# A separate byte offset for each stage's split activations in an fp32r matmul kernel

## The chip, the cores and the metric

The kernel runs on one core of a Trainium2 chip, in one launch. The metric is device time in microseconds. Before the change it is 2463.53 us, the median of two runs (2461.48 and 2465.57).

## What is computed

The reference runs two blocks, one after the other, on a sequence of 256 tokens with 1024 features in float32. The first block is a gated mixer (spatial gating, a depthwise convolution of width 31, a multi-scale pool) with a feed-forward layer. The second has two layers: a retention mixer and a latent attention mixer, each followed by a "peer" layer that scores all 16,384 experts densely in this kernel. Nearly all of the work is projections:

```python
proj = hn @ w_in[i]                                   # 1024 -> 8192
f_gate, f_up = jnp.split(hn @ w_ffn_in[i], 2, axis=-1)  # 1024 -> 2 * 2816
f = (jax.nn.silu(f_gate) * f_up) @ w_ffn_out[i]
...
q, k, v, g = jnp.split(x @ w_in, [RET_HK, 2 * RET_HK, 2 * RET_HK + RET_HV], axis=-1)
...
h = jax.nn.gelu(jnp.einsum('thkd,td->thk', u[eidx], xb), approximate=False)
return jnp.einsum('thk,thkd->td', gate * h, v[eidx])
```

## The kernel before

**Weights.** All weights are a list of 797 units of 128 x 1024 float32 in the order in which they are used (PLAN, L32). A unit comes from HBM into one of four `raw` buffers (issue_dma, L134), ScalarE copies it into one of three `whi` buffers as fp32r (issue_hi, L143), and VectorE subtracts the two into one of three `wlo` buffers (issue_split, L154). So a weight is a high part and a low part, both fp32r.

**Activations.** They are split in the same way into a high part `[:, 0]` and a low part `[:, 1]`, in a tile of 2 x 8 x 256 values (two halves of 8 KB in each partition, a k-step every 1 KB). The tile named `hl` lies in the pool `keep`, in one buffer with the tag "hl" that eight stages use in turn (new_hl, L441, and two tiles written out at L710 and L749).

**Two kinds of matmul.** A product is three matmuls: high x high, high x low, low x high.

- Feature-major stages (lin_fm, L234, and the expert loop at L1315) call mm3. The weight's 128 columns are the stationary operand, and a k-step of `hl`, 256 columns, streams through:

```python
220    def mm3(ps, w, x, start, stop):
...
222        nc.tensor.matmul(ps, w[0], x[0], start=start, stop=False, skip_group_check=True)
223        nc.tensor.matmul(ps, w[0], x[1], start=False, stop=False, skip_group_check=True)
224        nc.tensor.matmul(ps, w[1], x[0], start=False, stop=stop, skip_group_check=True)
```

- Token-major stages (lin_tm, L296) call tm_half. Here 128 columns of the activations are stationary and 512 columns of the weight stream:

```python
286        nc.tensor.matmul(ps[:, :n], xh, w[0][:, o:o + n], start=first, stop=False, skip_group_check=True)
287        nc.tensor.matmul(ps[:, :n], xh, w[1][:, o:o + n], start=False, stop=False, skip_group_check=True)
288        nc.tensor.matmul(ps[:, :n], xl, w[0][:, o:o + n], start=False, stop=last, skip_group_check=True)
```

Each matmul loads its own stationary operand (the rows of PEld), while the matmul before it streams.

**Addresses.** Pools are laid out by the sizes of their tiles. In each partition, `hl` begins at byte 14,848, which is 29 x 512. The weight buffers (`raw`, `whi`, `wlo`) begin at byte 32,320 and follow each other every 4,096 bytes; each lies 64 bytes past a multiple of 512. A weight's 128 columns are 512 bytes and a k-step of `hl` is 1,024, so modulo 512 the weight is always 64 bytes ahead of `hl`, in all stages. The other split tiles have places of their own: `fhl`, `yhl`, `ohl` and the expert loop's `ch` and `cl` lie 64 bytes past a multiple of 512, as the weights do; `hl2`, `hl4`, `hl5`, `hlp` and `cqhl` lie on one.

**What sets the order.** The order on every engine is that of the program text (manual_schedule); the only work between the matmuls of a stage is what `pump` (L170) takes from background generators. The stages that use `hl`, in order: w_conv, w_pin, w_u, w_v and w_gate (one tile), w_pgr, w_co, w_fi, then r_qk, r_v and r_g (one tile), then p_q0 with the 128 units of p_u0 (one tile), m_in, and p_q1 with p_u1 (one tile).

Of the kernel before, what the change touches and what calls it, by code (L numbers as in the profile page):

```python
# [11 lines left out]
F32R = mybir.dt.float32r  # L12
# [7 lines left out]
P = 128  # L20
T = 256
D = 1024
KD = D // P
# [69 lines left out]
def fused_kernel(ctx: ExitStack, tc: tile.TileContext, a: dict, out: bass.AP):  # L93
# [4 lines left out]
    keep = ctx.enter_context(tc.tile_pool(name="keep", bufs=1))  # L98
# [244 lines left out]
    def table_ready(func=AF.Sqrt):  # L343

        nc.scalar.activation(out=small("rt", 1), in_=eps_t[:, 0:1], func=func)
# [92 lines left out]
                nc.tensor.matmul(psb[b][k // 4][:, (k % 4) * P:(k % 4 + 1) * P], hm[:, k, b * P:(b + 1) * P], ident,  # L438
                                 start=False, stop=False, is_transpose=True, skip_group_check=True)

    def new_hl():  # L441
        return keep.tile([P, 2, KD, T], F32R, tag="hl", name="hl")

    class LnTail:

# [98 lines left out]
    issue_split(1)  # L544
    spread(dgs, bA)
    table_ready(AF.Sigmoid)
    hl = new_hl()
    hn32 = mx.tile([P, KD, T], F32, tag="hn32", name="hn32")

    def pr_x(k):  # L550
# [141 lines left out]
    def mk_branch(gi, first, last=None):  # L692
        def ev(f, ps):
            if first and f == 0:
                held["m"] = mx.tile([P, KD, T], F32, tag="v", name="merged")
            merged = held["m"]
            if first:
                nc.vector.tensor_tensor(out=merged[:, f, :], in0=ps, in1=gates[:, gi * 8 + f, :], op=ALU.mult)
                return
            t = tmp(mx, "brt")  # L700
            nc.vector.tensor_tensor(out=t, in0=ps, in1=gates[:, gi * 8 + f, :], op=ALU.mult)
            nc.vector.tensor_tensor(out=merged[:, f, :], in0=merged[:, f, :], in1=t, op=ALU.add)
            if last is not None and f > 0:
                late(f - 1)
        return ev
# [1 line left out]
    def late(f):  # L707
        split_to(hl5[:, 0, f, :], hl5[:, 1, f, :], held["m"][:, f, :])

    hl3 = keep.tile([P, 2, KD, T], F32R, tag="hl", name="hl3")  # L710
    br_s = mk_branch(0, True)

    def ev_sgo(f, ps):
# [18 lines left out]
    for gi in range(4):  # L732
        for f in range(2):
            c = 2 * gi + f
            gp = bank(c % 4)[:, :T]
            for k in range(2):
                t = gi * 4 + f * 2 + k
# [8 lines left out]
    drain_bg()  # L746


    hl3 = keep.tile([P, 2, KD, T], F32R, tag="hl", name="hl3b")  # L749
    cvt = {}  # L750

    def pr_conv1(c):
# [35 lines left out]
    lin_tm("w_out", of_fm(hl5), KD, after=rt1.after, warm=WRM)  # L788


    hl = new_hl()
    sqs = {}
    sqp = {}

# [117 lines left out]
    for f in range(8):  # L912
        for k in range(2):
            t = 2 * f + k
# [15 lines left out]
        split_to(hlp[:, 0, k, :], hlp[:, 1, k, :], h2[:, k, :])  # L930

    h3 = hm
    hl = new_hl()

    def ev_pleg(f, ps):
        t = ff.tile([P, T], F32, tag="ft", name="plt", bufs=3)
# [109 lines left out]
    ret_t(16)  # L1046
    ret_t(17)
    yl = rt.tile([P, 2, 1024], F32, name="yl")
    hl = new_hl()
    lt = LnTail(yl, "lm_g0", "lm_b0", hm, hl)  # L1050
    lin_tm("r_o", of_fm(yhl), 16, each=lambda k: 4 <= k < 8 and scale_h(k - 4), mid=add_h, after=lt.after, warm=WRM)

# [333 lines left out]
    def after0(X):  # L1386
        flat = X.rearrange("p a b -> p (a b)")
        y = flat[:, 0:2048].rearrange("p (b f) -> p b f", b=2)
        hl_ = new_hl()
        hl2_box["lt"] = LnTail(y, "lf_g0", "lf_b0", hm, hl_)  # L1390
        hl2_box["hl"] = hl_
        return hl2_box["lt"].after
# [5 lines left out]
    def angles():  # L1398
# [9 lines left out]
        yield from sincos(ang, sn2.rearrange("p b o f -> p (b o f)"), cs2.rearrange("p b o f -> p (b o f)"), keep, 64, 2.5, 2.5)  # L1408

    PE0, X = peer(0, hl, lt, [RT, TB], after0, beside_v=[angles()])  # L1410
    lt, hl = hl2_box["lt"], hl2_box["hl"]

# [171 lines left out]
            att_out(k + 1)  # L1584

    yl = ml.tile([P, 2, 1024], F32, name="yl")
    hl = new_hl()
    lt = LnTail(yl, "lm_g1", "lm_b1", hm, hl)
    lin_tm("m_o", of_fm(ohl), 8, each=att_each, mid=add_h, after=lt.after, warm=WRM)

# [142 lines left out]
```

## Time and profile before

| | us |
|---|---|
| median of the two runs | 2463.53 |
| the profiled execution | 2461.35 |
| its span, first to last instruction | 2459.3 |
| TensorE busy (PE) | 2423.2 |
| weight loads (PEld) | 2205.6 |
| VectorE busy | 1792.0 |
| ScalarE busy | 1285.0 |

The profile records for each matmul a start and a modelled end. In a stream, matmuls overlap, so that one lasts 276 ns or more while a new one starts every 113 ns or so; the distance from start to start is what the stream costs.

### The profile page before, as it was taken

Reading aid. Unit: us, or ns where it says so; the run is one execution under the profiler, and the core shown is the slowest. Engines: PE = TensorE matmul, PEld = TensorE weight load, DVE = VectorE, ACT = ScalarE, POOL = GpSimd, SP = SyncE. Lnnn points to the kernel's source line nnn. Section 1 sums busy time; section 2 is a strip of 40 time slices with the busy share of each in tenths; the row PEclk is TensorE's granted clock in tenths of the full one; section 3 lists DMA queues with packets and bytes.
Section 4 is the critical chain, followed back from the end, with each engine's and each line's share of the span. In section 5 each row is a group of like instructions: output and inputs, shape, how many; then the busy total and the mean of one; then the engine's idle time right before and its main releaser. Section 6 shows DMA issues by size and latency. Waiting matters only on the chain. (4 is left out here: it accounts for less than half of the span.)

```text
span 2459.3 us, 43069 instructions
## 1 busy us (share of the span) xinstructions
PE 2423.2 (99%) x16839; PEld 2205.6 (90%) x16839; DVE 1792.0 (73%) x3456; ACT 1285.0 (52%) x2175; POOL 4.9 (0%) x13
## 2 busy tenths in 40 slices
PE   8999999999999999999999999999999999999998
PEld 8899989889889999999878888779999999888886
DVE  7988767667657988889655555667978898555555
ACT  5444555564455555555455545645565555454554
POOL 0000000000000000000000000000000000000000
PEclk9999999999999999999999999999999999999999
DMA  6645555546354555545555555424555455655553
GB/s 205 221 143 172 180 161 189 189 163 197 127 182 165 175 188 176 172 164 172 188 188 194 192 196 183 135 86 164 191 195 166 168 168 172 213 191 194 196 191 128
DMA packets 119772, 432.66 MB, mean 176 GB/s; under 512 B 13808, under 2 KB 14192, under 8 KB 119184
## 3 DMA queue, kind: packets, MB, share of 16 engines
q1 hardware_dynamic: 118832, 425.84, 52.4%
q0 software_dynamic: 736, 4.06, 0.5%
q8 instruction: 132, 2.16, 0.3%
q14 instruction: 72, 0.59, 0.1%
HBM read 428.81 MB, written 1.05 MB: 175 GB/s over the span
## 5 line engine op out<-in xcount | busy, mean ns | idle before, releaser
L165 DVE TENSOR_TENSOR wlo<-raw,whi 128x1024 fp32r<-128x1024 f32 (+1 forms) x797 | 968.5, 1217 | 497.0 <-ACT whi L150 494.4
L150 ACT ACTIVATE whi<-raw 128x1024 fp32r<-128x1024 f32 (+1 forms) x797 | 839.8, 1055 | 686.0 <-PE bank L288 446.9
L222 PE MATMUL bank<-hl,whi 128*128 128x256 f32 x2080 | 586.0, 282 | 4.1 <-ACT hl L552 3.3
L223 PE MATMUL bank<-hl,whi 128*128 128x256 f32 x2080 | 578.6, 278 | 0.3
L224 PE MATMUL bank<-hl,wlo 128*128 128x256 f32 x2080 | 578.0, 278 | 0.3 <-DVE wlo L165 0.3
L286 PE MATMUL bank<-whi,ch 128*128 128x512 f32 x1024 | 398.9, 390 | 2.0 <-ACT ch L324 2.0
L288 PE MATMUL bank<-whi,cl 128*128 128x512 f32 x1024 | 398.8, 389 | 0.3 <-DVE cl L325 0.2
L287 PE MATMUL bank<-wlo,ch 128*128 128x512 f32 x1024 | 398.4, 389 | 0.0
L222 PEld LDWEIGHTS bank<-hl,whi 128*128 128x128 f32 x2080 | 392.6, 189 | 5.0 <-ACT hl L552 3.6
L223 PEld LDWEIGHTS bank<-hl,whi 128*128 128x128 f32 x2080 | 392.1, 189 | 1.4 <-DVE hl L467 0.5
L224 PEld LDWEIGHTS bank<-hl,wlo 128*128 128x128 f32 x2080 | 391.9, 188 | 1.2 <-DVE wlo L165 0.9
L222 PE MATMUL lps<-hl,whi 128*128 128x256 f32 x1208 | 342.6, 284 | 1.0 <-ACT fhl L836 0.6
L224 PE MATMUL lps<-hl,wlo 128*128 128x256 f32 x1208 | 336.8, 279 | 0.5 <-DVE wlo L165 0.5
L223 PE MATMUL lps<-hl,whi 128*128 128x256 f32 x1208 | 336.7, 279 | 0.0
L286 PEld LDWEIGHTS bank<-whi,ch 128*128 128x128 f32 x1024 | 192.2, 188 | 42.4 <-ACT ch L324 2.8
L288 PEld LDWEIGHTS bank<-whi,cl 128*128 128x128 f32 x1024 | 192.2, 188 | 41.9 <-DVE cl L325 1.9
L223 PEld LDWEIGHTS lps<-hl,whi 128*128 128x128 f32 x1208 | 229.0, 190 | 0.3
L222 PEld LDWEIGHTS lps<-hl,whi 128*128 128x128 f32 x1208 | 227.2, 188 | 1.8 <-ACT fhl L836 0.7
L224 PEld LDWEIGHTS lps<-hl,wlo 128*128 128x128 f32 x1208 | 227.0, 188 | 0.7 <-DVE wlo L165 0.7
L287 PEld LDWEIGHTS bank<-wlo,ch 128*128 128x128 f32 x1024 | 192.2, 188 | 39.4
L1304 ACT ACTIVATE gel<-bank 128x16 f32<-128x16 f32 (+31 forms) x152 | 43.3, 285 | 178.8 <-PE bank L224 178.8
L1306 ACT ACTIVATE X<-bank 128x256 f32<-128x256 f32 (+25 forms) x246 | 76.6, 311 | 106.7 <-PE bank L224 106.6
(411 smaller groups left out, 2981.9 us busy)
## 6 DMA issues: line engine op xcount, KB each, us to landing
raw<-in_p_u_dram SPq DMA_DIRECT2D x256, 512.0 KB, 3.3
raw<-in_p_v_dram SPq DMA_DIRECT2D x256, 512.0 KB, 3.5
raw<-in_w_fi_dram SPq DMA_DIRECT2D x44, 512.0 KB, 4.3
raw<-in_p_q_dram SPq DMA_DIRECT2D x32, 512.0 KB, 3.7
raw<-in_w_gate_dram SPq DMA_DIRECT2D x24, 512.0 KB, 3.3
raw<-in_w_fo_dram SPq DMA_DIRECT2D x22, 512.0 KB, 4.1
raw<-in_w_conv_dram SPq DMA_DIRECT2D x16, 512.0 KB, 4.4
raw<-in_r_qk_dram SPq DMA_DIRECT2D x16, 512.0 KB, 3.4
```

Source lines behind the costliest of these rows:

```text
L150: nc.scalar.activation(out=hi[:, :c], in_=raws[j][:, :c], func=AF.Copy)
L165: nc.vector.tensor_tensor(out=lo[:, :c], in0=r[:, :c], in1=hi[:, :c].bitcast(F32), op=ALU.subtract)
L222: nc.tensor.matmul(ps, w[0], x[0], start=start, stop=False, skip_group_check=True)
L223: nc.tensor.matmul(ps, w[0], x[1], start=False, stop=False, skip_group_check=True)
L224: nc.tensor.matmul(ps, w[1], x[0], start=False, stop=stop, skip_group_check=True)
L286: nc.tensor.matmul(ps[:, :n], xh, w[0][:, o:o + n], start=first, stop=False, skip_group_check=True)
L287: nc.tensor.matmul(ps[:, :n], xh, w[1][:, o:o + n], start=False, stop=False, skip_group_check=True)
L288: nc.tensor.matmul(ps[:, :n], xl, w[0][:, o:o + n], start=False, stop=last, skip_group_check=True)
L1304: nc.scalar.activation(out=gl_[:, 0:td], in_=ps[:, 0:td], func=AF.Gelu)
L1306: nc.scalar.activation(out=X[:, e, td:], in_=ps[:, td:T], func=AF.Gelu)
```

## The change

`new_hl` takes an offset in bytes. The tile becomes 512 bytes larger (128 values more), and the stage's 2 x 8 x 256 values begin at that offset in it. The two tiles written out at L710 and L749 now come from `new_hl` too. Everything that is laid out behind `hl`, the weight buffers among it, moves by 512 bytes. The instructions on each engine, their order, their shapes and what they wait for are those of before.

```diff
-    def new_hl():
-        return keep.tile([P, 2, KD, T], F32R, tag="hl", name="hl")
+    def new_hl(off, name="hl"):
+
+        t = keep.tile([P, 2 * KD * T + 128], F32R, tag="hl", name=name)
+        return t[:, off // 4:off // 4 + 2 * KD * T].rearrange("p (a k t) -> p a k t", a=2, k=KD)
...
-    hl = new_hl()
+    hl = new_hl(128)
...
-    hl3 = keep.tile([P, 2, KD, T], F32R, tag="hl", name="hl3")
+    hl3 = new_hl(288, "hl3")
...
-    hl3 = keep.tile([P, 2, KD, T], F32R, tag="hl", name="hl3b")
+    hl3 = new_hl(416, "hl3b")
...
-    hl = new_hl()
+    hl = new_hl(320)
...
-    hl = new_hl()
+    hl = new_hl(256)
...
-    hl = new_hl()
+    hl = new_hl(448)
...
-        hl_ = new_hl()
+        hl_ = new_hl(0)
...
-    hl = new_hl()
+    hl = new_hl(384)
```

What this makes of the distance, modulo 512 bytes, from the streaming operand to the one that is being loaded:

| stages | offset | feature-major: weight minus `hl`, before / after | token-major: `hl` minus weight, before / after |
|---|---|---|---|
| w_conv, w_u, w_gate; w_pin, w_v | 128 | 64 / 448 | 448 / 64 |
| w_pgr | 288 | 64 / 288 | |
| w_co | 416 | 64 / 160 | |
| w_fi | 320 | 64 / 256 | |
| r_qk, r_g; r_v | 256 | 64 / 320 | 448 / 192 |
| p_q0, p_u0 | 448 | 64 / 128 | |
| m_in | 0 | | 448 / 448 |
| p_q1, p_u1 | 384 | 64 / 192 | |

## Rows read from the trace of the kernel before

**Rows 1.** The page: busy us and share; granted TensorE clock in 40 slices.
```profile
PE 2423.2 (99%) x16839; PEld 2205.6 (90%) x16839; DVE 1792.0 (73%) x3456; ACT 1285.0 (52%) x2175; POOL 4.9 (0%) x13
...
PEclk9999999999999999999999999999999999999999
```

**Rows 2.** Windows inside w_fi and p_u0: start:end length, busy of each engine, clock, DMA.
```profile
340.00:440.00 100.00, 100.00 (x851) 100.00 (x851) 72.20 (x108) 50.66 (x72) 0.00 (x0) 1.00 0.58 190
825.00:850.00 25.00, 25.00 (x223) 25.00 (x222) 25.00 (x108) 13.84 (x20) 0.00 (x0) 1.00 0.59 195
```

**Rows 3.** Groups by line, 340 to 440 us: busy us, mean ns | idle before.
```profile
L223 PE MATMUL lps<-hl,whi 128*128 128x256 f32 x284 | 79.8, 281 | 0.0
```

**Rows 4.** Groups by line, 825 to 850 us.
```profile
L223 PE MATMUL bank<-hl,whi 128*128 128x256 f32 x74 | 20.4, 276 | 0.0
```

**Rows 5.** Windows by stage, L224 alone: PE busy (x), PEld busy (x), clock, DMA.
```profile
14.80:60.80 46.00, 36.05 (x128) 25.03 (x128) 0.95 0.57 183
...
318.80:450.40 131.60, 98.81 (x352) 66.08 (x352) 1.00 0.56 179
...
643.40:701.70 58.30, 35.65 (x128) 24.18 (x128) 1.00 0.44 144
753.60:818.50 64.90, 44.53 (x160) 30.06 (x160) 1.00 0.49 163
818.50:1190.00 371.50, 274.77 (x993) 186.34 (x992) 1.00 0.54 178
1659.10:1724.30 65.20, 44.69 (x161) 30.16 (x161) 1.00 0.47 162
1724.30:2096.50 372.20, 274.98 (x992) 186.31 (x992) 1.00 0.54 177
sum 1280.10, PE 908.93 PEld 615.84; mean PE 82.63 PEld 55.99
```

**Rows 6.** Groups by line, 60.8 to 82.8 us (w_pin, `hl` stationary).
```profile
L288 PE MATMUL bank<-whi,hl 128*128 128x512 f32 x32 | 12.6, 394 | 0.0
L287 PE MATMUL bank<-wlo,hl 128*128 128x512 f32 x32 | 12.5, 392 | 0.0
L286 PE MATMUL bank<-whi,hl 128*128 128x512 f32 x32 | 12.4, 388 | 0.0
```

**Rows 7.** Groups by line, 450.5 to 510 us (w_fo, `fhl` stationary).
```profile
L287 PE MATMUL bank<-wlo,fhl 128*128 128x512 f32 x88 | 34.2, 389 | 0.0
```

**Rows 8.** Order of time in p_q0: start us, duration us, what.
```profile
769.79 0.36 PE L222 MATMUL lps<-hl,whi 128*128 128x256 f32 x1
769.99 0.28 PE L223 MATMUL lps<-hl,whi 128*128 128x256 f32 x1
...
772.70 0.61 PE L1111 MATMUL ax<-X,q 128*128 128x128 f32 x4
773.06 0.37 PE L222 MATMUL lps<-hl,whi 128*128 128x256 f32 x1
773.26 0.28 PE L223 MATMUL lps<-hl,whi 128*128 128x256 f32 x1
...
773.62 0.28 PE L223 MATMUL lps<-hl,whi 128*128 128x256 f32 x1
...
774.18 0.28 PE L222 MATMUL lps<-hl,whi 128*128 128x256 f32 x1
```

**Rows 9.** Order of time in p_u0: float16 matmuls of 128 columns.
```profile
1004.50 0.22 PE L1275 MATMUL ax<-o,ohh 128*128 128x128 f16 x1
...
1005.17 0.22 PE L1275 MATMUL ax<-o,ohh 128*128 128x128 f16 x1
```

**Rows 10.** Order of time after w_out: float16 matmuls of 384 columns.
```profile
312.21 4.07 PE L294 MATMUL ax<-idle 128*128 128x384 f16 x24
```

**Rows 11.** Waits of PE, by what ended them: us in total, times, longest.
```profile
PE bank L222 <- ACT hl L552: 3.3, 1, 3.3
```

## The prediction
> **What bounds the kernel now.** [...] Then the waits of TensorE: the longest in total is 3.3 us, once, at the start [rows 11]. So there is next to no idle time to win, and the time is the number of matmuls by the distance from one start to the next. That distance is what the change can touch, since it moves no instruction and changes no shape.
>
> Next I cut windows out of long streams of mm3. In w_fi, 851 matmuls stand in 100 us; a window also counts those that reach in from before it (two or three, since one lasts 281 ns), so about 849 starts, 117.8 ns each [rows 2, 3]. In p_u0, 223 stand in 25 us, less 2.4, so 113.3 ns each [rows 2, 4]. The same 256 columns, the same engine, the same clock of 1.00, no idle time before them, and the same 64 bytes of distance: two rates. The duration column shows which one a stretch runs at, 281 or 276 ns. I call them the dear and the cheap rate; they are 4.5 ns apart.
>
> The order of time in p_q0 shows how a stretch comes to its rate. After an interruption by other matmuls (L1111) the first L222 starts 200 ns before the next matmul. From 769.99 to 772.70 the next 23 matmuls run at the dear rate, 117.8 ns. After the next interruption the dear rate holds for three matmuls, and from 773.62 to 774.18 five take 0.56 us, 112 to 113 ns each [rows 8]. So a rate, once found, lasts until something interrupts the stream; w_fi kept the dear one for a whole 100 us [rows 2, 3]. I read this as two operand streams, the columns that flow through and the next stationary operand, that settle into a relation in which they hinder each other or don't.
>
> That addresses have a part in it is seen in the token-major stages. With `fhl` stationary, 64 bytes past a multiple of 512 like the weights, the groups show 389 ns [rows 7], in the two other lines of that stage as well. With `hl` stationary, 64 bytes before them, the three lines show 388, 392 and 394 [rows 6]. The mean of these is 391.3, 2.3 ns more, with the same shape and no wait.
>
> **The change, part by part.** It removes and adds no instruction, wait or transfer. Three things move.
>
> First, the larger tile shifts all that lies behind it by 512 bytes. Distances modulo 512 among the weights and the other split tiles stay; I cost this at nothing, because within one stage the k-steps move by 1,024 bytes against weights that move by 512, and w_fi holds one rate through all of them [rows 2, 3]. So larger multiples of 512 don't show.
>
> Second, the writes into `hl` begin at other bytes, in the same shape. They lie beside TensorE's work except at a stage's start, where the largest wait for one of them is 3.3 us in all [rows 11]. I cost this at nothing; a write that gets slower by a tenth, in eight stage starts of that size at the very most, would cost 2.6 us.
>
> Third, the distance between the two operands changes in each stage. What can be won is the dear part. From the windows by stage: L224 is busy 98.81 us for 352 matmuls in w_fi, 280.7 ns each, so a cheap one is 276.2 by the 4.5 ns above. Eleven stages that stream `hl` hold 3,275 matmuls of L224 (seven of the rows stand there, and the sum over all): 908.93 us less 3,275 x 0.2762 = 904.6 leaves 4.4 us, and by three for the three lines of mm3, 13 us [rows 5]. Of that, w_fi alone is (98.81 - 352 x 0.2762) x 3 = 4.8; p_u1 gives 274.98 - 992 x 0.2762 = 1.0, by three 3.0; p_u0 0.5, by three 1.5; p_q0 and p_q1 together 0.6, by three 1.7; w_conv 0.7, by three 2.1, part of which are the clock of 0.95 and the waits of its start. The token-major stages with `hl` stationary are 384 matmuls (96 in w_pin, 96 in w_v, 192 in r_v) by 2.3 ns, 0.9 us [rows 6, 7]; they get distances of 64 and 192 in place of 448. So the most that can be won by bringing all to the cheap rate is 13 + 0.9 = 14 us.
>
> No row shows a feature-major stream at another distance than 64, so the price of the new distances has to be bounded. From below: all cheap, -14 us. From above: all dear, the rate that w_fi shows. The 9,825 matmuls of the eleven stages have about 13 us / 4.5 ns = 2,900 at 117.8 ns already; the other 6,900 by 4.5 ns are +31 us. Between the two I take -11 us: the dear rate is gone wherever it now lasts (w_fi, the long runs in p_q and p_u), and what stays is a few matmuls after each interruption and the start of w_conv. I choose near the lower end because 389, 389, 389 against 388, 392, 394 [rows 6, 7] shows that a distance without the dearer rate exists, and because most of `hl`'s stream, 6,900 of 9,825, is at the cheap rate even now, so a settled stream is cheap more often than not.
>
> What would be late next if TensorE gets faster? In the window of p_u0 at the cheap rate VectorE is busy for all of 25.00 us, and TensorE still shows no gap there; w_fi, which would go from 117.8 to 113.3 ns, has VectorE at 72% and the DMA share at 0.58, against 0.59 in that window [rows 2]. So the feed keeps up, and the 11 us come through to the end.
>
> The sum: the profiled execution of 2461.35 us (2.05 around the span of 2459.3) less 11 is 2450.3. It lies 2.2 us below the median of the two runs, 2463.53; against that median the forecast is 2452.5.
>
> [...]
>
> **The rivals.**
>
> *Addresses don't decide (no change).* The two rates stand at one and the same distance, 64, in w_fi and p_u0 [rows 2], and an interruption changes the rate where no address changes [rows 8]. Then the rate is a matter of timing, the new offsets only deal the same cards again, and the time is 2463.5, give or take some 4 us. Against it speak rows 6 and 7.
>
> *The new distances are worse (slower).* The mechanism is the dear rate as the settled state: with another distance, the load of the next weight meets the stream at more of its length, and a stretch that now falls back to the cheap rate after three matmuls [rows 8] stays dear as w_fi does [rows 2, 3]. Its place is p_u0 and p_u1, with 3 x (993 + 992) = 5,955 of the 9,825 matmuls [rows 5]. The change turns from gain to loss when more than about 2,900 of the matmuls that are cheap now become dear, as many as can be cured. If both p_u stages turn dear and the rest stays, their 5,955 less some 1,000 that stand at 117.8 ns already ((1.5 + 3.0) us / 4.5 ns) by 4.5 ns are +22 us: 2486. If all turn dear, 2494. For it: seven distances are new, and nothing in the trace has tried them. Against it: the token-major stages at 448, bytes that no row shows as good, lose only 2.3 of 391 ns.
>
> *The cheap rate isn't the floor (much faster).* Float16 matmuls of 128 columns start every 0.67 us / 12 = 55.8 ns [rows 9]. The 24 of 384 columns take 4.07 us to the end of the last, whose tail is some 0.33, so (4.07 - 0.33) / 23 = 163 ns each [rows 10]. The line through both gives 109.3 ns for 256 columns. If what fp32r pays above that, 4.0 ns at the cheap rate, came from the distance of 64 as well, 9,825 x 4.0 = 39 us more would go: 2452.5 less 39 is 2413. Against it: with `fhl`, at another distance (0) and with twice the columns, the duration is 389, and 389 less the same tail of 163 is 226, twice 113 [rows 7]. An excess that goes with the columns at two distances looks like the price of fp32r itself.
>
> [...]
>
> **How the numbers follow.** Forecast, 2440 to 2459: 0.50. No change, 2459 to 2468: 0.25. Worse distances, 2468 to 2495: 0.20. A lower floor, 2405 to 2440: 0.05. The likeliest is the first, 2452.5. For the range I leave out the lower floor's best part and the worst third of the slower case: 2438 to 2482. A measurement of this kernel tells about 2% from no change, 49 us, and hardly any of these cases reaches that: only the full lower floor (2413) does on the fast side, 0.03, and on the slow side only a rate above the dear one, which no settled stretch shows, 0.03. Within 2%: 0.94.
>
> **What would show it right or wrong.** Right: the mean of L222 to L224 in w_fi falls from 281 to 276, the L224 sum over the stages falls from 908.9 to 905 or 906, the three lines of w_pin show 389 alike, and the stages without `hl` (w_fo, the p_v loops) keep their 389. If 281 stays in w_fi and the stretches of 117.8 ns come back in p_q0 at the same places, addresses don't decide. Means of 278 to 281 or more in p_u0 and p_u1 are the slower case, and means under 275 the lower floor. The forecast as a whole is wrong if stages that don't use `hl` change, or if TensorE's idle time grows by more than a microsecond or two.

## The result, and the profile after

The changed kernel takes 2494.15 us, the median of two runs (2493.69 and 2494.61), against 2463.53. The ratio is 1.0123, 95% interval 1.0104 to 1.0141: it is slower by 1.2%. The forecast was 2452.5, with a range that ended at 2482.

The page of the changed kernel shows the loss on TensorE, and only there:

```profile
PE 2454.6 (99%) x16839; PEld 2237.1 (90%) x16839; DVE 1796.7 (72%) x3456; ACT 1285.5 (52%) x2175; POOL 4.9 (0%) x13
```

Against [rows 1], the same 16,839 matmuls are busy for 31.4 us more; the span grew by 32.5, from 2459.3 to 2491.8. TensorE's idle time, the span less the busy time, is 37.2 us against 36.1, and its longest wait 3.6 us against 3.3 [rows 11]. So waits account for about 1 us, and the rest is that the matmuls stand farther apart. Windows in the middle of w_fi, early in p_u0 and early in p_u1 of the changed kernel (start:end length, busy and count of PE, PEld, DVE, ACT, POOL, then clock, DMA share, GB/s):

```profile
344.00:444.00 100.00, 100.00 (x836) 100.00 (x835) 71.07 (x106) 49.73 (x70) 0.00 (x0) 1.00 0.58 189
831.00:856.00 25.00, 25.00 (x213) 25.00 (x213) 25.00 (x108) 11.37 (x18) 0.00 (x0) 1.00 0.61 198
1760.00:1785.00 25.00, 25.00 (x215) 25.00 (x214) 24.31 (x111) 13.48 (x19) 0.00 (x0) 1.00 0.58 187
```

Less the 2.4 matmuls that reach in from before, these are 100 us / 833.6 = 120.0 ns from start to start in w_fi, 25 / 210.6 = 118.7 in p_u0 and 25 / 212.6 = 117.6 in p_u1. Before, w_fi had 117.8 and p_u0 113.3 [rows 2]; a window early in p_u1 of the kernel before, which the prediction did not look at, was dear already (25 / 211.6 = 118.1, with one longer gap in it):

```profile
1728.00:1753.00 25.00, 25.00 (x214) 25.00 (x214) 25.00 (x107) 11.70 (x19) 0.00 (x0) 1.00 0.58 196
```

In other words w_fi has a third rate, above both that were seen before, and this part of p_u0 has lost the cheap one. What p_u1 lost lies later and is read from the sums and the interruptions below.

The windows by stage, L224 alone, answer to [rows 5] (w_fi, p_u0, p_u1, and the sum over the eleven stages):

```profile
322.40:456.20 133.80, 99.47 (x352) 67.50 (x352) 1.00 0.55 176
...
826.10:1212.60 386.50, 280.13 (x996) 187.27 (x995) 1.00 0.53 172
...
1747.10:2129.90 382.80, 277.01 (x992) 185.60 (x992) 1.00 0.53 173
sum 1313.60, PE 917.50 PEld 616.38; mean PE 83.41 PEld 56.03
```

The window of p_u0, the row that begins at 826.10, went from 371.5 to 386.5, that of p_u1 from 372.2 to 382.8, that of w_fi from 131.6 to 133.8. The stages r_qk and r_g have a distance of 320 now and ran as at 64, as the table below shows.

The token-major stage w_pin has `hl` stationary, now 64 bytes past the weights in place of 64 before them, and w_fo has `fhl`, which kept its place (groups by line, busy us, mean ns | idle before):

```profile
L288 PE MATMUL bank<-whi,hl 128*128 128x512 f32 x32 | 12.6, 394 | 0.0
L286 PE MATMUL bank<-whi,hl 128*128 128x512 f32 x32 | 12.6, 394 | 0.0
L287 PE MATMUL bank<-wlo,hl 128*128 128x512 f32 x32 | 12.6, 394 | 0.0
```
```profile
L287 PE MATMUL bank<-wlo,fhl 128*128 128x512 f32 x87 | 33.9, 389 | 0.0
```

All three lines of w_pin now show what only the worst of them did [rows 6]; w_fo is unchanged [rows 7].

For a sum over stages I took each matmul with `hl` as an operand and added up the distances from its start to the next matmul's start, from the same traces:

| stage | before | after | difference |
|---|---|---|---|
| w_conv, w_u, w_gate (offset 128) | 106.1 | 108.0 | 1.9 |
| w_pin, w_v (128, token-major) | 43.9 | 44.8 | 0.9 |
| w_pgr (288) | 5.8 | 5.9 | 0.1 |
| w_co (416) | 23.2 | 23.9 | 0.7 |
| w_fi (320) | 127.7 | 129.8 | 2.1 |
| r_qk, r_g (256) | 90.3 | 90.4 | 0.1 |
| r_v (256, token-major) | 44.6 | 44.6 | 0.0 |
| p_q0, p_u0 (448) | 402.4 | 417.2 | 14.8 |
| m_in (0, token-major) | 16.8 | 16.8 | 0.0 |
| p_q1, p_u1 (384) | 403.4 | 414.1 | 10.7 |
| sum | 1264.1 | 1295.4 | 31.3 |

So 31.3 of the 32.5 us lie in the stages that stream `hl`, and 25.5 in the two peer layers. The rest is in other stages at 64, above all 0.6 in the stage with `hlp`. The small differences are not safe: the kernel before, profiled once more (last experiment below), differs from its own first profile by 2.2 us in w_conv to w_gate with no change at all. The 14.8 and 10.7 us of the peer layers lie far outside what they show at distance 64 in five profiles, 402.4 to 404.1 us.

**Where the cheap rate went.** In p_u0 and p_u1 float16 matmuls (L1275 and L1276 before, two lines lower after) interrupt the stream 64 times. One interruption of p_u1 before, in order of time, and the same after:

```profile
1905.34 0.22 PE L1276 MATMUL ax<-o,ohl 128*128 128x128 f16 x1
...
1906.82 0.28 PE L222 MATMUL bank<-hl,whi 128*128 128x256 f32 x1
...
1908.18 0.28 PE L222 MATMUL bank<-hl,whi 128*128 128x256 f32 x1
```
```profile
1902.13 0.22 PE L1278 MATMUL ax<-o,ohl 128*128 128x128 f16 x1
...
1903.66 0.28 PE L222 MATMUL bank<-hl,whi 128*128 128x256 f32 x1
...
1905.07 0.28 PE L222 MATMUL bank<-hl,whi 128*128 128x256 f32 x1
```

The two last rows of each are twelve matmuls apart: 1.36 us before, 113.3 ns each, and 1.41 after, 117.5. I read the starts after all 64 interruptions in this way. Before, 64 of 64 streams came back at 113.3 ns. After, none did: the 32 of p_u0 (distance 128) ran at 118.7 ns in the mean, the 32 of p_u1 (distance 192) at 117.8.

### The profile page after: what moved, and what is told of

Read it like the earlier page. It is cut to its first block, busy times and chain, and to the rows that moved or that the text cites. A ratio compares the mean times of both kernels' runs of the same rounds, so it can differ in the third digit from the quotient of the medians.

```text
span 2491.8 us, 43069 instructions
## 1 busy us (share of the span) xinstructions
PE 2454.6 (99%) x16839; PEld 2237.1 (90%) x16839; DVE 1796.7 (72%) x3456; ACT 1285.5 (52%) x2175; POOL 4.9 (0%) x13
## 5 line engine op out<-in xcount | busy, mean ns | idle before, releaser
L222 PE MATMUL bank<-hl,whi 128*128 128x256 f32 x2080 | 592.2, 285 | 4.5 <-ACT hl L554 3.6
L223 PE MATMUL bank<-hl,whi 128*128 128x256 f32 x2080 | 585.1, 281 | 0.3
L224 PE MATMUL bank<-hl,wlo 128*128 128x256 f32 x2080 | 583.9, 281 | 0.5 <-DVE wlo L165 0.5
L224 PEld LDWEIGHTS bank<-hl,wlo 128*128 128x128 f32 x2080 | 391.1, 188 | 0.8 <-DVE wlo L165 0.7
L224 PE MATMUL lps<-hl,wlo 128*128 128x256 f32 x1208 | 338.9, 281 | 0.4 <-DVE wlo L165 0.4
L224 PEld LDWEIGHTS lps<-hl,wlo 128*128 128x128 f32 x1208 | 228.6, 189 | 0.7 <-DVE wlo L165 0.6
```

## The experiments

Theory A: the distance from the streaming operand to the stationary one that is loaded meanwhile decides, modulo 256 bytes, which rates exist and into which one a stream falls (the second half did not hold, as the last experiment shows). Its rivals: B, only the place of `hl` itself counts; C, the larger tile or the shift by 512 bytes costs something; D, each stage's timing decides and the offsets only deal it again. In every run only addresses differ.

**The tile without the offsets.**

```diff
-    hl = new_hl(128)
+    hl = new_hl(0)
...
-    hl = new_hl(384)
+    hl = new_hl(0)
```

(All eight calls.) 

> The larger tile stays (512 bytes more, all behind it shifted by 512), but all eight offsets are 0, so every stage has its old distance of 64. Theory A (the distance modulo 256 from the streaming operand to the next stationary one decides): the time of before, 2463.5 us within 3 us; w_fi at 117.8 ns from start to start, p_u0 and p_u1 mostly at 113.3. Rival C (the larger tile or the shift by 512 costs something itself): some of the 31 us stay, 2475 to 2494.

Measured: 2461.62 us, ratio 0.9999 (0.9990 to 1.0009). Rival C falls. Two windows were a surprise, in w_fi and early in p_u0:

```profile
341.00:441.00 100.00, 100.00 (x885) 100.00 (x884) 75.24 (x112) 52.97 (x75) 0.00 (x0) 1.00 0.62 198
821.00:846.00 25.00, 25.00 (x215) 25.00 (x214) 25.00 (x108) 11.62 (x19) 0.00 (x0) 1.00 0.61 199
```

The first holds 882.6 starts, 113.3 ns each, where the kernel before had 117.8 at the same distance. The second line shows the reverse in p_u0: 215 matmuls early in the stage, the dear rate, where the kernel before had 223 [rows 2].

**All offsets 256.** The same eight lines with 256. 

> All eight offsets are 256, so the distance is 320 in every stage. After the change r_qk and r_g already had 320 and kept the time they had at 64. Theory A with a period of 256 bytes: the time of before, 2463.5 us within 3 us, with the two rates in the same places. With a period of 512 bytes or more: other rates in w_fi and the two p_u stages, and a time that differs by 5 us or more.

Measured: 2463.97 us, ratio 1.0002 (0.9991 to 1.0013), w_fi at 117.7 and the peer layers at 403.4 and 403.7 us by the sum of starts. So 320 is as good as 64, as a period of 256 bytes, or of a part of it, would have it.

**The weights moved in place of `hl`.** A tile of `keep` between `hl` and the weights grows by 128 bytes:

```diff
-    sc2 = keep.tile([P, 144], F32, name="sc2")[:, 0:128].rearrange(...)
+    sc2 = keep.tile([P, 176], F32, name="sc2")[:, 0:128].rearrange(...)
```

> The kernel before, with hl where it was, but 128 bytes more in front of the weight buffers and all that is laid out behind them: the distance becomes 192 in each stage that streams hl, while hl keeps its place. Theory A: all of these stages settle at 117.8 ns, as w_conv, w_u and p_u1 do after the change at 192: p_u0 and p_u1 some 11 us more each, r_qk and r_g 2 to 3, w_conv to w_gate 2, w_fi nothing, the token-major stages at 64 some 1.5: 2488 to 2493 us. Rival B (what counts is where hl itself begins, and a start off a multiple of 256 bytes streams at a higher price): the time of before, 2463.5, as hl hasn't moved.

Measured: 2485.72 us, ratio 1.0097 (1.0080 to 1.0114). The window in w_fi:

```profile
344.00:444.00 100.00, 100.00 (x884) 100.00 (x884) 75.25 (x112) 52.91 (x75) 0.00 (x0) 1.00 0.62 198
```

Early windows of the peer layers (215 matmuls in both) do not tell 192 from 64, since the run with all offsets 0 has 215 there too; the sums of starts do.

`hl` lies where it always did, and yet p_q0 with p_u0 takes 414.1 us and p_q1 with p_u1 414.0, which is what p_q1 with p_u1 takes in the changed kernel at the same distance of 192 (414.1). w_pin shows 394 ns in all three lines, as it does after the change at the same token-major distance of 64. Rival B falls: it is the relation of the two operands. The time is 2.3 us under the range that I expected; w_fi went the other way: 884 matmuls, less 2.4, are 113.4 ns each. So 192 has the cheap rate too; w_fi kept it for 100 us, while the interrupted peer layers fell into 117.8 after every one of the 64 interruptions.

**The peer layers exchanged.**

```diff
-    hl = new_hl(448)
+    hl = new_hl(384)
...
-    hl = new_hl(384)
+    hl = new_hl(448)
```

> The changed kernel with the offsets of the two peer layers exchanged: p_u0 at 384 (distance 192), p_u1 at 448 (distance 128). Theory A: the settled rates go with the offset, p_u0 at 117.8 ns throughout and p_u1 between 117 and 120, their three mm3 lines together some 4 us less in p_u0 and 4 us more in p_u1 than after the change; in all 2494 within 4 us. Rival D (each stage's own timing decides, the offsets only deal it again): the rates do not go with the offset.

Measured: 2494.12 us in one run. The windows in p_u0 and p_u1:

```profile
830.00:855.00 25.00, 25.00 (x215) 25.00 (x214) 25.00 (x110) 11.81 (x18) 0.00 (x0) 1.00 0.58 195
1748.00:1773.00 25.00, 25.00 (x213) 25.00 (x212) 25.00 (x110) 11.84 (x18) 0.00 (x0) 1.00 0.59 193
```

They are those of the changed kernel, exchanged. By the sum of starts p_q0 with p_u0 takes 414.1 us (117.8 in undisturbed stretches), p_q1 with p_u1 417.2 (118.8, between 117 and 120). Against the changed kernel that is 3.1 less and 3.1 more, and the values go with the offset to the tenth of a microsecond. For the difference between 128 and 192 in the peer layers rival D falls.

**One load of three at distance 0.** Two pads move `wlo` by 192 bytes and all behind it by 256:

```diff
+                if not j:
+                    wst.tile([P, 48], F32, tag="gap", name="gap")
                 lo = wst.tile([P, 1024], F32R, tag="wlo", ...)
...
+    sm.tile([P, 16], F32, tag="gap", name="gap", bufs=1)
```

> The kernel before with the low parts of the weights (wlo) alone moved by 192 bytes, so that their distance to hl is 0 modulo 256, while the high parts (whi) stay at 64; all behind is shifted by 256 bytes. Theory A in its sharper form (each load of a stationary operand that meets the stream costs one slot of 16 columns, 6.67 ns, as all three do at distance 0, 120.0 ns): one load of three is at 0, so the settled rate of the hl stages is 115.6 ns or, where the dear state of 64 adds to it, up to 120; never 113.3. In the p_v loops, where ch and cl stay at 64 and the streaming wlo is now at 0, one of three lines meets its load at 64, so 228.9 ns in place of 226.7, some 3.4 us more in each p_v loop. A rival (the three lines settle together, by the distance of the high parts alone): 113.3 and 226.7 stay.

Measured: 2503.09 us in one run. The first window lies in the p_v0 loop, the second in r_qk (1300 to 1400 us, 575 to 600 us):

```profile
1300.00:1400.00 100.00, 100.00 (x438) 82.05 (x437) 56.24 (x73) 52.38 (x78) 0.00 (x0) 1.00 0.59 191
575.00:600.00 25.00, 25.00 (x207) 25.00 (x206) 19.75 (x34) 11.57 (x18) 0.00 (x0) 1.00 0.55 178
```

In p_v0 this kernel has 438 matmuls in 100 us, the kernel before 443 in the same window:

```profile
1300.00:1400.00 100.00, 100.00 (x443) 82.81 (x442) 57.73 (x74) 49.94 (x75) 0.00 (x0) 1.00 0.58 194
```

By the starts 226.7 ns became 228.9, the value expected when one load of three pays 6.67 ns, the step from 113.3 to the 120.0 of distance 0 (6.67 / 3 = 2.2). In the `hl` stages no settled stretch ran at 113.3, as theory A says, but none ran at 115.6 either; most ran at 117.8 (both peer layers, w_fi). And r_qk ran at 122.2 and w_co at 120.4 in the mean, over the 120 that I had given as the end. So the sharper form gave the right price in the p_v loops, and in the `hl` stages its ceiling of 6.67 ns for each load, 120.0 ns, doesn't hold.

**Other distances.** Three runs with other offsets in the same eight calls.

> The changed kernel with other offsets, to read the settled rate at distances not tried yet: w_conv, w_u and w_gate at distance 48, w_fi at 80, r_qk and r_g at 96, p_u0 at 72, p_u1 at 56. Theory A (slots of 64 bytes, modulo 256): all rates lie between 113.3 and 120.0, near 64 the cheap rate of 113.3 is still reached, and at 96 it is on the way to the 117 to 120 of 128. A rival (what counts is whole multiples of 64 bytes, and any other start costs more by itself): all of these lie above 118.

> As the run before, with w_conv, w_u and w_gate at distance 96, w_fi at 48, r_qk and r_g at 80, p_u0 at 112, p_u1 at 16. Theory A: rates rise from 64 towards 128 and towards 0, so 80 is cheaper than 96, 96 than 112, and 16 is near the 120 of distance 0. If a distance lets no stretch fall into the dear state, its stage is as cheap as 113.3 all through: p_u at 396 us or less for its 3,456 matmuls in place of 402 to 404.

> As the two before, on the far side: w_conv, w_u and w_gate at distance 224, w_fi at 208, r_qk and r_g at 144, p_u0 at 176, p_u1 at 240. Theory A: 192 has both rates (113.3 and 117.8, by the run with the weights moved), so 176 and 208 lie between these, 224 and 240 rise towards the 120 of distance 0, and 144 towards the 117 to 120 of 128.

Measured, in one run each: 2506.60, 2491.58 and 2484.33 us. The mean distances from start to start in undisturbed stretches (those with no start-to-start distance more than 25 ns over 113.3 within five matmuls on either side), of these runs and the others (those that are told below too):

| distance modulo 256 | feature-major, ns (stage) |
|---|---|
| 0 | 120.0 (w_fi) |
| 16 | 117.2 (p_u1) |
| 32 | 118.3 (w_pgr, 29 matmuls) |
| 48 | 118.5 (w_conv), 119.2 (w_fi) |
| 56 | 120.0 (p_u1) |
| 64 | 113.3 and 117.8; each peer layer 114.1 to 114.7 |
| 72 | 120.0 (p_u0) |
| 80 | 119.3 (w_fi), 119.2 (r_qk) |
| 96 | 118.1 (w_conv), 117.8 (r_qk) |
| 112 | 117.5 (p_u0) |
| 128 | 118.8 (p_u0; p_u1 when exchanged) |
| 144 | 114.2 (r_qk), 113.4 (w_fi), 113.6 (p_u0, p_u1) |
| 160 | 120.0 (w_co) |
| 176 | 118.9 (p_u0) |
| 192 | 117.8 (p_u0, p_u1), 113.4 (w_fi); w_conv 117.8, but 113.3 in the run with the peer layers exchanged |
| 208 | 118.3 (w_fi) |
| 224 | 116.8 (w_conv) |
| 240 | 115.2 (p_u1), 117.0 (r_qk), 118.2 (w_conv) |

My expectation that rates rise smoothly away from 64 was wrong. The rival (any distance that is no whole multiple of 64 lies above 118) falls as well: 144 is at 113.4 to 114.2, 16 at 117.2, 112 at 117.5 and 224 at 116.8. Eight bytes to either side, 56 and 72, are as bad as 0 (120.0 ns each), while 144, far away, is as good as 64. The law has a fine structure that these runs don't resolve: 56 and 72 are also the only two at which `hl` doesn't begin on a multiple of 16 bytes, and I did not try that apart from the distance. No settled rate lies under 113.3 at any distance. Token-major stages read 226.7 at 0, 228.9 at 192, and 233.3 at 32, 64 and 112. They too have two rates at one distance: w_out, whose distance is 192 in the kernel before, ran at 229.0 in the first profile of the kernel before and at 233.4 in the second.

**The peer layers alone undone.** The changed kernel with 0 in place of 448 and 384. 

> The changed kernel with the two peer layers alone back at offset 0 (distance 64). If the stages add up, as their sums in the traces do (p_q0 with p_u0 417.2 us after against 402.4 before, p_q1 with p_u1 414.1 against 403.4), 25.5 of the 31 us go: 2467 to 2471 us, some 5 us over the kernel before, which stand in w_fi (2.1), w_conv to w_gate (1.9, and 0.9 in w_pin and w_v) and w_co (0.7). A rival (an early stage hands its relation of load and stream on to the later ones, so that the peer layers stay dear): above 2480.

Measured: 2472.72 us, ratio 1.0041 (1.0027 to 1.0056), 1.7 us over what I expected. The peer layers are back at 404.1 and 403.4 us, and w_fi keeps its 129.8. So stages add up, and the two offsets explain 21 of the 31 us by the medians, 23.8 by the sums of starts (831.3 less 807.5). The rival falls.

**Trying to beat both.** First with 144 and 240 in the long stages, and m_in at distance 0:

```diff
-    hl = new_hl(320)
+    hl = new_hl(176)
...
-    hl = new_hl(256)
+    hl = new_hl(80)
...
-    hl = new_hl(448)
+    hl = new_hl(176)
```

(w_conv at 80, w_pgr and w_co at 0, m_in at 64, the second peer layer at 176 as well.) 

> The best two of the distances tried so far beside 64, to see if one beats it: 144 in w_fi and both peer layers, 240 in w_conv, w_u, w_gate and in r_qk, r_g; 64 in w_pgr and w_co; m_in, which is token-major alone, at distance 0 like w_fo. r_qk and r_g at 144 ran at 114.2 ns, p_u1 at 240 at 115.2. If 144 has only the cheap rate, p_q and p_u take 395 to 400 us each in place of 402 to 404 and w_fi 123 in place of 127.7, and the kernel 2445 to 2458. If it has dear stretches as 64 has, or others at other matmuls between: 2460 to 2475.

Measured: 2462.33 us, ratio 1.0002 (0.9993 to 1.0012). The gain at 144 (401.7 in each peer layer, 123.4 in w_fi) was given back at 240: 109.7 us in w_conv to w_gate and 92.1 in r_qk and r_g, against 106.1 and 90.3 in the first profile of the kernel before (its second has 108.3 and 91.8). One good reading at 240 had not been enough. Then 144 alone:

```diff
-    hl = new_hl(320)
+    hl = new_hl(176)
...
-    hl = new_hl(448)
+    hl = new_hl(176)
...
-    hl = new_hl(384)
+    hl = new_hl(176)
```

(0 in the five other calls.) 

> A version that may beat both: distance 144 in w_fi and in both peer layers, 64 everywhere else as before. By the stage sums of the runs so far (p_q with p_u 401.7 us at 144 against 402.4 to 404.1 at 64; w_fi 123.4 at 144 against 127.7 or 123.4 at 64, by the rate it falls into), 2 to 8 us less than the kernel before: 2454 to 2460 us, a ratio of 0.997 to 0.999. If the distance of the earlier stages shifts the rate that the later ones fall into, no difference.

Measured: 2458.43 us, ratio 0.9977 (0.9968 to 0.9987), as expected. The windows in w_fi, p_u0 and p_u1:

```profile
341.00:441.00 100.00, 100.00 (x885) 100.00 (x884) 75.22 (x112) 52.93 (x75) 0.00 (x0) 1.00 0.62 198
819.00:844.00 25.00, 25.00 (x223) 25.00 (x222) 25.00 (x108) 12.50 (x19) 0.00 (x0) 1.00 0.60 201
1724.00:1749.00 25.00, 25.00 (x222) 25.00 (x222) 25.00 (x106) 12.54 (x19) 0.00 (x0) 1.00 0.61 200
```

All three long streams stand at the cheap rate, 113.3 to 113.8 ns. It beats the kernel before by 0.23% and the changed one by 1.4%. The gain in the peer layers is small, 0.7 to 2.4 us each against the five profiles at 64, and lies in the stretches that are dear at 64 as a rule, such as the early windows above. How much of the gain in w_fi belongs to 144 is open: it was cheap in both runs at 144, but also in one of four profiles at 64 (or 320) and in the one at 192.

**The kernel before, once more.** Nothing changed. 

> The kernel before, unchanged, profiled once more, to see if its rates are fixed by the program or fall differently in each execution. If the timing at a stage's start decides which of the two rates of distance 64 a long stream falls into, some stage differs from the first profile: w_fi at 113.4 ns (123.4 us) in place of 117.7 (127.7 us), or r_qk and r_g, w_co or the plg stage. If the program's addresses alone decide, the stage sums are those of the first profile within 0.3 us.

Measured: 2469.21 us in this one execution, 7.9 over the first profile. The sums of starts differ in w_conv to w_gate (108.3 against 106.1) and in r_qk with r_g (91.8 against 90.3); those of w_fi are alike (127.6 and 127.7), and those of the peer layers nearly (403.8 and 403.7 against 402.4 and 403.4). In r_qk the undisturbed starts lie 117.8 ns apart where they had lain 113.3. So at distance 64 the addresses alone don't fix the rate. That timing has the other say, so that an execution that starts a stage a little differently falls into the other of the two rates, is my reading. With the distance unchanged at 64, w_fi was cheap in the run with all offsets 0 (123.4 us) and dear in both profiles of the kernel before.

How little the starts differ where the two rates part is seen early in the peer layers. There, in all ten streams at distance 64 (or 320) of five profiles, one start lies 171 to 174 ns after the last, about 5.6 us after two others that came late. In nine it is 173 or 174 ns, and the stream that had been cheap is dear from there to the next interruption, some 56 us later. In one it is 171 ns, and the stream stays cheap: p_u0 in the first profile, the window of [rows 2].

## Why the prediction was wrong

Point by point:

- *The bound is TensorE, and the start-to-start distance is what the change touches.* Right: idle time grew by 1.1 us only, and 31.3 of 32.5 us stand in the streams of `hl`.
- *The shift by 512 bytes costs nothing, and so do the writes into `hl`.* Right for the shift: 0.9999 with all offsets 0. The writes were not tested by themselves; the run that moved the weights and left `hl` in place lost as much in p_u1 as the change did, so nothing is left for them there.
- *Larger multiples of 512 don't show.* Right (0.9999 with all offsets 0), and 256 doesn't either (1.0002 with all offsets 256).
- *The feed keeps up.* Not tested by the change, since nothing got faster; in the version with 144 it did (w_fi at 113.3 ns with VectorE at 75%).
- *"I choose near the lower end because ... a distance without the dearer rate exists, and because most of `hl`'s stream, 6,900 of 9,825, is at the cheap rate even now"*. This is the step that failed. That 70% of the stream was cheap was no property of settled streams at any distance; it belonged to the distance of 64, about half of it to the streams after interruptions by float16 matmuls: 64 of 64 came back cheap there, 0 of 64 at 128 and 192. The window of p_u0 from which the cheap rate was read [rows 2] was itself a lucky one: at the same distance nine of ten such early streams were dear. The token-major rows [rows 6, 7] showed that distance matters; they did not show that a new one is as good. In fact 64 is, with 144, the best of the ten distances at which a peer layer ran. The forecast term of -11 us became +31.
- *"From above: all dear, the rate that w_fi shows"*, +31. The term was mis-sized: w_fi's 117.8 is not the ceiling. At distance 0 it settled at 120.0, p_u0 at 128 on 118.8. That the total came to the rival's 2494 all the same is partly chance: r_qk and r_g, 768 of the 9,825 matmuls, stood at 320, which is 64 modulo 256, and did not turn dear, while w_fi and p_u0 went above 117.8.
- *The rival "the new distances are worse"* had the right place and, in the main, the right course: streams that came back cheap after an interruption (64 of 64 before) stay dear (all 64 after). That the load meets the stream at more of its length was my guess at the cause; no run shows it. By the sums of starts p_u0 and p_u1 gave 13.4 and 9.8 us, 23.2 where it had said 22. I gave it 0.20. Nothing in the trace of before favoured a new distance over the old one, and with one distance tried and seven new the chances of the two signs should have been the other way round.
- *The rival "addresses don't decide"* is half right: at 64 the same program falls into either rate from one execution to the next (r_qk at 113.3 and 117.8 ns). It is wrong in that no timing brought 113.3 at 128, or after the interruptions at 192, and in that the run that moved the weights and not `hl` took 2485.72 us in place of 2462.32 with the same instructions, by the relation of the two operands' addresses alone.
- *The rival "the cheap rate isn't the floor"* is not borne out: no settled rate at any of the 18 distances lay under 113.3 ns. The 109.3 ns that I estimated from the float16 rows [rows 9, 10] was seen at none of them.
- I read the rate off the duration column (281 or 276 ns). In p_u1 after the change the durations are 279 and 280 ns at 117.8 from start to start, so this column doesn't tell the rates apart in general; counts in a window and starts do. In w_conv I had read 2.1 us of dear rate out of durations; its undisturbed starts lie 113.3 ns apart, so there was none to win.

What stays open is why the law looks as it does: why 144 is as good as 64, why 56 and 72 are not, and why the cheap rate went on after a start at 171 ns and the dear one began after a start at 173. The runs show relations, not the memory's inside.

## What to carry to other kernels

Where fp32r matmuls stream back to back and each loads its own stationary operand, the addresses of the two operands relative to each other, modulo 256 bytes, were worth up to 6% of the stream in this kernel (113.3 against 120.0 ns): measure the start-to-start distance at each candidate place, and keep the one that is still cheap after the interruptions the stage really has. A stage that shows two rates at one address tells that a better state exists, not that another address has it; a good reading at one stage (240 here), or in one execution of one stage (p_u0 in [rows 2]), needs a second one before it is used. Bound an untried address from above by more than the worst row seen.

## What had not been expected of the hardware

- The same program, with the same addresses, ran w_conv to w_gate in 106.1 us in one execution and 108.3 in another; w_fi kept one rate through a window of 100 us, 117.8 ns in the kernel before and 113.3 with all offsets 0. A single start 173 ns after the last, in place of 171, was followed by the dear rate in place of the cheap one.
- The steps between rates are alike: 113.3, 117.8 and 120.0 ns for 256 columns, 226.7, 228.9 and 233.3 for 512, which are 0, 4.4 or 6.7, and 0, 2.2 or 6.7 ns above the lowest. A third of 6.7 is 2.2 and two thirds are 4.4: as if one, two or all three of a product's loads paid 6.7 ns each. This is a reading, not shown; means between these values (114.2 to 119.3) and one of 122.2 stand in the runs as well. The 16 columns that I put for 6.67 ns in the run with one load of three at distance 0 are an estimate, by 107 ns for 256 columns in the float16 rows [rows 9, 10].
- Float16 matmuls of 384 columns start every 163 ns, those of 128 every 55.8 [rows 9, 10]: 107 ns for 256 columns more, 0.42 ns a column. A line through the two leaves 2.2 ns that don't go with the columns (55.8 less 128 x 0.419, and 163 less 384 x 0.419), an estimate from two sizes. For fp32r 226.7 ns are twice 113.3, so nothing is left over there, and a column takes 0.443 ns: the excess over float16, 6%, grows with the columns.
